# Decay matrices from a stationary mask, scores computed with the chunk matrices, modulation sums gathered by 32x32 transposes, and tokens loaded first

## The chip, the core and the metric

The kernel runs as one program on one core of a Trainium2 chip. The metric is the device time of one execution in microseconds (us), the median of several runs. The engines of the core are named as in the profile: PE (matrix multiplication; PEld is its weight load), DVE (vector), ACT (activation), POOL (GpSimd), SP (it only issues DMAs here), and sixteen DMA engines that all queues share.

## The reference, cut to what matters

Two layers over 256 latent tokens and 256 context tokens of width 2048, all in float32. Layer 0 mixes by eight gated-DeltaNet heads, in both directions of time, beside eight neighbourhood-attention heads; layer 1 mixes by a short gated convolution. Each layer ends in a SwiGLU network with 5632 hidden columns. Before each mixer and each SwiGLU the tokens are normalised and modulated by rows that come from a condition vector.

```python
sh1, sc1, g1, sh2, sc2, g2 = jnp.split(jax.nn.silu(c) @ ada_w[l] + ada_b[l], 6, axis=-1)
h = modulate(x_lat, norm_mix[l], sh1, sc1)
...
# gated delta rule, chunks of tokens (g, beta: one value per token and head, in two directions)
gc = jnp.cumsum(g, axis=-1)
decay = jnp.exp(jnp.where(lower_incl, gc[..., :, None] - gc[..., None, :], -jnp.inf))
m = jnp.where(i[:, None] > i[None, :], jnp.einsum('bhnid,bhnjd->bhnij', kb, k) * decay, 0.0)
t_inv = lax.linalg.triangular_solve(eye + m, ...)                 # inverse of each chunk's matrix
...
a_intra = jnp.where(lower_incl, jnp.einsum('bhnid,bhnjd->bhnij', q, k) * decay, 0.0)
# scan over chunks: v_new = u - w S;  S' = S exp(g_last) + k_dec^T v_new;  o = q_dec S + a_intra v_new
...
s_loc = jnp.einsum('brqhd,brjkhd->bhrqjk', qg, kg) * scale + bias # neighbourhood attention, bias from rpb
```

The context tokens give only the start state of the delta rule and extra keys and values; the output is the latent stream.

## The kernel before, in words

**Numbers.** A float32 product of large matrices is made from three products of "float32r" parts: each weight block of 128 x 1024 is copied to `whi` (ACT) and the rest subtracted into `wlo` (DVE), and the tokens are held as a high and a low part as well. `tm_stream` (tokens stationary, weights moving in 512 columns, lines 291 to 302) and `fm_stream` (weights stationary, 256 tokens moving, lines 317 and 321) run such a product over sixteen (or 44) blocks `k` of 128 rows. One `k` is one "step". Small products of the delta rule use plain float32 matmuls.

**Order.** Each engine runs its own instructions in a fixed order. That order is written at build time by a planner (`schedule_with_timeline_sim=True`), which plays the program through with its own estimates of durations and takes what the program names first. `Pump` draws a certain number of steps of a side job for each step of a stream. `plan` holds four pieces of the delta rule that are put into the program at the step numbers of `P_INV`; steps are counted over the streams QB (2 x 16 steps), KB and VB (2 x 32 steps).

**The start.** `start_block(b)` (b from 0 to 7) loads 4.2 MB of layer 0's modulation weights into four `araw0` tiles and sums them over the condition vector on PE (line 533). `token_stats` loads all tokens (`xn`, 4.2 MB, line 569), takes squares on ACT and scales by the root mean square on DVE (line 576). `start_tokens(b)` turns the sums into shift and scale of two blocks of 128 features, transposes the tokens' features, modulates them and splits them into `h_hi` and `h_lo`; the first two streams (`C_KA`, through `both`) take two steps each beside every block.

**The delta rule.** `gates` makes `g_t`, `beta` and their exponentials. `decay(d, tt, q)` gives exp of the sums of `g` between two tokens of a chunk for four heads: a mask times `g_t` (DVE, line 834), four float32 matmuls against the opposite mask (line 838), exp on ACT (line 840). `chunk_matrices(seq)` is called for the context (`seq` 1) and, inside `second_inverse`, for the latents (`seq` 0): it makes k.k products (`pG`, line 870), times decay and beta (`nt`, line 874), cuts out the 32x32 diagonal blocks (`dgs`: DVE transposes, line 880, and ACT copies), the off-diagonal ones (POOL copies, line 884, and ACT copies), and solves all diagonal blocks at once by 31 dependent pairs of DVE operations; the result goes through a DRAM tile `dz` and comes back as `xd` and `xdT`. `inverses` joins them by small matmuls (lines 962 to 979). `latents`, at step `P_INV[3]`, calls the second inverse of the latents, then `latent_scores(q)` for two groups of four heads (q.k products, line 1070, eight more calls of `decay`, two DVE products each, lines 1073 and 1074, into `AT`), then `latent_quad(q)`, which runs `scan` (lines 1000 to 1044).

**Beside and after it.** Eight attention heads (`na_scores`, `na_values`, lines 1180 to 1212); each head first loads its bias rows `br` (two DMAs, one buffer) and adds the band mask into `bq` (DVE, line 1183). The stream ZA follows, whose result `zst` goes to the DRAM tile `zd` by a DMA on SP (line 1220). `latent_out(q)` normalises the delta rule's output and splits it into `yhi`, `ylo`. The stream of `ev_w_out` takes its sixteen `k` in the order `YO` = (2, 0, 1, 3): attention heads 0 to 3, delta heads 0 to 3, delta heads 4 to 7, attention heads 4 to 7.

**Later modulation.** `ada_job` adds weight rows times the condition into `acc` (128 x 1024, DVE, line 346), one row block per step, beside the streams of SwiGLU 0 (8 column blocks), of layer 1's mixer (4) and SwiGLU 1 (2). At the end of a block it sums `acc` over the 128 partitions: `acc` is split into `ah` (ACT) and `al` (DVE), sixteen matmuls with the one-column mask `pick` (line 355) give 8 x 128 sums, ACT copies them, and for the kinds "sh" and "sc" a transpose turns them back to columns.

Of the kernel before, what the change touches and what calls it, by code (L numbers as in the profile page):

```python
# [42 lines left out]
P_INV = (30, 32, 79, 80)  # L43
# [65 lines left out]
def body(tc, x, c, ctx, c_ctx, ada_w, ada_b, norm_mix, norm_ffn, ffn_w_gate, ffn_w_up, ffn_w_down,  # L109
# [224 lines left out]

    def ada_job(pool_, l, seg, kind, gamma=None):

        wr = ada_w[l].rearrange("(k p) n -> p k n", p=128)
        for blk in range(2):
# [11 lines left out]
            ah = pool_.tile([128, 1024], F32R, name="ah", tag="ah", bufs=1)  # L350
            al = pool_.tile([128, 1024], F32R, name="al", tag="al", bufs=1)
            split(ah, al, acc, DVE)
            for f in range(8):
                for a in (ah, al):
                    PE.matmul(p[0:8, 0:128], pick[:, 7 - f:15 - f], a[:, f * 128:(f + 1) * 128],
                              start=f == 0 and a is ah, stop=f == 7 and a is al)
# [5 lines left out]
            pc = smt()  # L362
            transpose(pc[:, 0:8], g)
            ada_done(l, seg, kind, gamma, fs_, pc[:, 0:8])
# [344 lines left out]

    sums = start_block(0)  # L710
    token_stats()
# [106 lines left out]
    gates()  # L818
    abstk.close()
# [11 lines left out]
    def decay(d, tt, q):  # L831

        gm = g2("gm")
        DVE.tensor_tensor(gm, C(("gt", "lt")[d])[:, None, :].to_broadcast([128, 4, 128]),
                          g_t[:, d, tt, q * 4:q * 4 + 4, None].to_broadcast([128, 4, 128]), op=OP.mult)
        pD = gdt()
        for i in range(4):
            PE.matmul(pD[:, i * 128:(i + 1) * 128], gm[:, i, :], C(("le", "ge")[d]), start=True, stop=True)
        em = g2("em")
        ACT.activation(em, pD.rearrange("p (i e) -> p i e", i=4), AF.Exp)  # L840
        return em
# [11 lines left out]
    def chunk_matrices(seq):  # L853
# [6 lines left out]
        for q in range(2):  # L860
# [3 lines left out]
            SP.dma_start(kTd[:, seq, q * 4:q * 4 + 4, :], kT)  # L864
            for ti in range(2):
                tok = slice(ti * 128, ti * 128 + 128)
                nt = gw.tile([128, 2, 4, 128], F32, name="nt", tag="lsol", bufs=1)
                pG = gdt()
                for i in range(4):
                    PE.matmul(pG[:, i * 128:(i + 1) * 128], kT[:, i, tok], kT[:, i, tok], start=True, stop=True)  # L870
                for d in range(2):
                    em = decay(d, t0 + ti, q)
                    for i in range(4):
                        DVE.scalar_tensor_tensor(nt[:, d, i, :], pG[:, i * 128:(i + 1) * 128],
                                                 beta[:, d, t0 + ti, q * 4 + i:q * 4 + i + 1], em[:, i, :],
                                                 op0=OP.mult, op1=OP.mult)
# [626 lines left out]
```

## Time and profile before

| | |
|---|---|
| median of 3 runs | 2819.64 us (2818.58 to 2827.38) |
| the profiled execution: its own time | 2823.79 us |
| its span (first to last instruction) | 2822.0 us |
| mean granted clock of PE | 0.989 |
| PE busy | 2719.8 us (96%) |
| DVE busy | 1920.1 us (68%) |
| ACT busy | 1301.9 us (46%) |
| POOL busy | 50.3 us (2%) |
| DMA | 680.78 MB, mean 241 GB/s |

Rough map of the span, by the first and last start of lines in the trace: the start to about 160 us; delta-rule preparation and the streams KA, QA and VA to about 388 us; QB, KB, VB, ZA, attention, scans and `ev_w_out` to about 925 us; SwiGLU 0 to about 1685 us; layer 1's mixer to about 2065 us; SwiGLU 1 to the end.

How to read the rows: a row of a timeline gives start, duration, engine, line, operation, output<-inputs, shape and count, and in brackets how long the engine was idle before and what ended that. A group row gives count, busy time in all, mean of one in ns, then idle time before. A row of a tile gives minimum, median and maximum in ns and the first and last start. A row of stretches gives busy time of each engine with its instruction count, then the granted PE clock, the DMA engines' busy share, and GB/s. A matmul's recorded duration includes its way through the array; what a matmul costs in a full queue is the distance from one start to the next.

### The profile page before, as it was taken

The numbers are of one execution on the slowest core, as the hardware profiler recorded it, in microseconds if no ns is written. First come the engines' busy times: TensorE is split into PE (matmuls) and PEld (weight loads), VectorE is DVE, ScalarE is ACT, GpSimd is POOL, SyncE is SP. The second block draws the span as 40 slices with busy tenths as digits, with TensorE's granted clock in tenths as the row PEclk, the third lists the DMA queues.
The fourth block names the chain that finished last, engine by engine and source line by source line (L and its number), as shares of the span: only waits on it lengthen the run. The fifth ranks groups of instructions, "written<-read, shape, count | busy, mean of one in ns | idle before, by whom it ended". The sixth has DMA issues, their size and how long they took to land.

```text
span 2822.0 us, 40405 instructions
## 1 busy us (share of the span) xinstructions
PE 2719.8 (96%) x15113; PEld 2277.5 (81%) x15113; DVE 1920.1 (68%) x2647; ACT 1301.9 (46%) x1943; POOL 50.3 (2%) x77
## 2 busy tenths in 40 slices
PE   5999989999999999999999999999999999999998
PEld 3799989887778788888888878878878888888886
DVE  2377768866767888776678667797678644445665
ACT  2267534322454544444455555444454444444554
POOL 0000100000000000000000000000000000000000
PEclk9999999999999999999999999999999999999999
DMA  9945578887758699987788647998559766656663
GB/s 342 325 135 157 148 234 259 270 250 226 213 200 285 208 333 340 345 291 255 264 283 286 197 154 275 333 327 286 186 196 326 247 193 186 187 188 215 190 192 126
DMA packets 286399, 680.78 MB, mean 241 GB/s; under 512 B 57209, under 2 KB 100833, under 8 KB 284795
## 3 DMA queue, kind: packets, MB, share of 16 engines
q1 hardware_dynamic: 281828, 668.73, 71.3%
q10 hardware_dynamic: 4375, 9.48, 0.9%
q8 instruction: 118, 1.93, 0.3%
q14 instruction: 78, 0.64, 0.1%
HBM read 657.63 MB, written 20.48 MB: 240 GB/s over the span
## 4 chain that ended last, share of the span: by engine, by line
PE 78%; DMA 10%; DVE 6%; ACT 3%; issue 2%; SPq 1%; DVEq 0%; POOL 0%; ACTq 0%
PE mm L294 19%; PE mm L291 19%; PE mm L292 19%; PE mm L321 7%; DMA araw<-in_ada_w_dram 5%; PE mm L300 2%; PE mm L301 2%; PE mm L302 2%; DVE wlo L243 2%; PE sm L191 2%; DMA raw<-in_od_w_in_dram 1%; PE sm L533 1%; DVE acc L346 1%; DVE acc L389 1%; PE gd L321 1%
## 5 line engine op out<-in xcount | busy, mean ns | idle before, releaser
L243 DVE TENSOR_TENSOR wlo<-raw,whi 128x1024 fp32r<-128x1024 f32 x800 | 971.1, 1222 | 436.8 <-ACT whi L172 430.9
L172 ACT ACTIVATE whi<-raw 128x1024 fp32r<-128x1024 f32 x800 | 842.2, 1059 | 825.6 <-PE mm L294 618.9
L292 PE MATMUL mm<-wlo,fhi 128*128 128x512 f32 x1232 | 472.4, 392 | 0.0
L291 PE MATMUL mm<-whi,fhi 128*128 128x512 f32 x1232 | 470.7, 396 | 0.0
L294 PE MATMUL mm<-whi,flo 128*128 128x512 f32 x1232 | 392.2, 392 | 0.1
L346 DVE SCALAR_TENSOR_TENSOR acc<-araw,cT,acc 128x1024 f32<-128x1024 f32 x224 | 287.3, 1283 | 130.2 <-DMA araw<-in_ada_w_dram 123.5
L294 PEld LDWEIGHTS mm<-whi,flo 128*128 128x128 f32 x1232 | 230.8, 188 | 51.1 <-DVE flo L1288 0.5
L292 PEld LDWEIGHTS mm<-wlo,fhi 128*128 128x128 f32 x1232 | 231.8, 188 | 48.7
L291 PEld LDWEIGHTS mm<-whi,fhi 128*128 128x128 f32 x1232 | 231.9, 188 | 48.2
L291 PE MATMUL mm<-whi,ahi 128*128 128x512 f32 x672 | 259.8, 392 | 0.0
L292 PE MATMUL mm<-wlo,ahi 128*128 128x512 f32 x672 | 259.3, 391 | 0.0
L294 PE MATMUL mm<-whi,alo 128*128 128x512 f32 x672 | 209.8, 392 | 0.0
L321 PE MATMUL mm<-hllo,whi 128*128 128x256 f32 x608 | 172.9, 289 | 0.0
L321 PE MATMUL mm<-hlhi,whi 128*128 128x256 f32 x570 | 161.7, 292 | 2.2 <-DVE hlhi L561 1.9
L175 ACT ACTIVATE ahi<-prodT 128x256 fp32r<-128x256 f32 x176 | 73.2, 417 | 194.6 <-PE mm L292 183.9
L389 DVE SCALAR_TENSOR_TENSOR acc<-araw,cT,acc 128x512 f32<-128x512 f32 x192 | 142.7, 747 | 29.1 <-DMA araw<-in_ada_w_dram 27.3
L321 PE MATMUL mm<-hlhi,wlo 128*128 128x256 f32 x570 | 157.8, 289 | 0.0
L292 PEld LDWEIGHTS mm<-wlo,ahi 128*128 128x128 f32 x672 | 126.2, 188 | 27.7
L294 PEld LDWEIGHTS mm<-whi,alo 128*128 128x128 f32 x672 | 126.1, 188 | 27.3
L291 PEld LDWEIGHTS mm<-whi,ahi 128*128 128x128 f32 x672 | 126.2, 188 | 27.1
L292 PE MATMUL mm<-wlo,dhi 128*128 128x512 f32 x336 | 126.4, 396 | 2.2 <-DVE wlo L243 2.2
L291 PE MATMUL mm<-whi,dhi 128*128 128x512 f32 x336 | 123.8, 397 | 0.6 <-DVE u_t L1428 0.6
(419 smaller groups left out, 4194.0 us busy)
## 6 DMA issues: line engine op xcount, KB each, us to landing
araw<-in_ada_w_dram SPq DMA_DIRECT2D x288, 512.0 KB
raw<-in_ffn_w_down_dram SPq DMA_DIRECT2D x176, 512.0 KB
raw<-in_ffn_w_gate_dram SPq DMA_DIRECT2D x160, 512.0 KB
raw<-in_ffn_w_up_dram SPq DMA_DIRECT2D x160, 512.0 KB
raw<-in_ev_w_in_dram SPq DMA_DIRECT2D x112, 512.0 KB
araw<-in_ada_w_dram SPq DMA_DIRECT2D x192, 256.0 KB
raw<-in_od_w_in_dram SPq DMA_DIRECT2D x96, 512.0 KB
raw<-in_ev_w_out_dram SPq DMA_DIRECT2D x32, 512.0 KB
```

The costliest lines, as they stand in the source:

```text
L172: ACT.activation(dst, src, AF.Copy)
L175: ACT.activation(hi, src, AF.Copy)
L191: return PE.transpose(dst, src, ident[:n, :n])
L243: last_lo[0] = DVE.tensor_tensor(lo, raw, hi, op=OP.subtract).ins
L291: PE.matmul(ps[ti][n], a, hi[:, n * 512:(n + 1) * 512], start=first, stop=False)
L292: PE.matmul(ps[ti][n], a, lo[:, n * 512:(n + 1) * 512], start=False, stop=False)
L294: last_mm[0] = PE.matmul(ps[ti][n], b, hi[:, n * 512:(n + 1) * 512], start=False, stop=False).ins
L300: PE.matmul(ps[ti][n], lh(t), hi[:, c_], start=False, stop=False)
L301: PE.matmul(ps[ti][n], lh(t), lo[:, c_], start=False, stop=False)
L321: last_mm[0] = PE.matmul(ps[f][:, n * 256:(n + 1) * 256], wt, mv(w, k), start=False, stop=i == len(ks) - 1 and g == len(group) - 1 and j = ...
L346: DVE.scalar_tensor_tensor(acc, raw, cT[:, k:k + 1], acc, op0=OP.mult, op1=OP.add)
L389: DVE.scalar_tensor_tensor(accs[n], raws.pop(i), cT[:, k:k + 1], accs[n], op0=OP.mult, op1=OP.add)
```

## The change

- **Tokens ahead.** `token_stats()` stands before `start_block(0)`.
- **Decay.** `g_t` is split once into `g_hi` and `g_lo` (float32r), and the two masks are copied to `past`. Each `decay` now makes two products of mask and `g` (one on DVE, one on POOL, float32r) and two float32r matmuls of 512 columns with `past` as the stationary part.
- **Scores with the chunk matrices.** `latent_scores` is gone. `chunk_matrices(0)` makes the q.k products beside its k.k products and uses the same decays, so 24 calls of `decay` become 16, and two loads of `kT` go; the load of `qT` moves with it. The decays are made before `pG`.
- **Steps.** `P_INV` goes from (30, 32, 79, 80) to (34, 36, 84, 86).
- **Later modulation.** `sum_parts` replaces split and `pick` matmuls: a DVE transpose of `acc` within 32x32 blocks, a DVE sum over 32, and four float32 matmuls of 8 columns with the mask `fold`. Kinds "sh" and "sc" need no transpose any more; "row" has one more copy and one transpose.
- **Attention bias.** `br` is gone, `bq` has three buffers and the mask is added in place.
- **ZA.** `zst` is written to `zd` from POOL's queue instead of SP's.

```diff
-P_INV = (30, 32, 79, 80)
+P_INV = (34, 36, 84, 86)
...
+    def sum_parts(dst, pool_, acc, n, tag, bufs):
+        at = pool_.tile([128, 4 * n, 32], F32, name="accT", tag=tag, bufs=bufs)
+        ar = pool_.tile([128, n, 4], F32, name="accR", tag="accR", bufs=bufs)
+        DVE.transpose(at.rearrange("p b r -> p (b r)"), acc)
+        DVE.tensor_reduce(ar.rearrange("p k b -> p (k b)"), at, axis=AX.X, op=OP.add)
+        for b in range(4):
+            PE.matmul(dst[b * 32:b * 32 + 32, 0:n], C("fold"), ar[:, :, b], start=True, stop=True)
...  (in ada_job)
-            split(ah, al, acc, DVE)
-            for f in range(8):
-                for a in (ah, al):
-                    PE.matmul(p[0:8, 0:128], pick[:, 7 - f:15 - f], a[:, f * 128:(f + 1) * 128],
-                              start=f == 0 and a is ah, stop=f == 7 and a is al)
-            g = pool_.tile([16, 128], F32, name="grow", tag="grow", bufs=1)[0:8]
-            acopy(g, p[0:8, 0:128])
+            sum_parts(p, pool_, acc, 8, "accT", 1)
             if kind == "row":
+                gc = pool_.tile([128, 8], F32, name="gcol8", tag="gcol8", bufs=1)
+                acopy(gc, p[:, 0:8])
+                pc = smt()
+                transpose(pc[0:8, 0:128], gc)
+                g = pool_.tile([16, 128], F32, name="grow", tag="grow", bufs=1)[0:8]
+                acopy(g, pc[0:8, 0:128])
...
-    sums = start_block(0)
     token_stats()
+    sums = start_block(0)
...
+    split(g_hi, g_lo, g_t)
+    for d in range(2):
+        acopy(past[:, d, :], C(("gt", "lt")[d]))
...  (in decay)
-        DVE.tensor_tensor(gm, C(("gt", "lt")[d])..., g_t[...].to_broadcast([128, 4, 128]), op=OP.mult)
-        for i in range(4):
-            PE.matmul(pD[:, i * 128:(i + 1) * 128], gm[:, i, :], C(("le", "ge")[d]), start=True, stop=True)
+        for i, (g_, e_) in enumerate(((g_hi, DVE), (g_lo, POOL))):
+            gm = gw.tile([128, 4, 128], F32R, name="gm", tag="m2", bufs=G2)
+            e_.tensor_tensor(gm, C(("le", "ge")[d])..., g_[...].to_broadcast([128, 4, 128]), op=OP.mult)
+            PE.matmul(pD, past[:, d, :], gm.rearrange("p i e -> p (i e)"), start=not i, stop=bool(i))
...  (in chunk_matrices)
+            if not seq:
+                qT = load_feat("qT", qTd[:, q * 4:q * 4 + 4, :], lg, 1)
+                ATs.append(lg.tile([128, 16, 128], F32, name="AT", tag="AT", bufs=2))
...
+                ems = [decay(d, t0 + ti, q) for d in range(2)]
...
+                if not seq:
+                    pK = gdt()
+                    for i in range(4):
+                        PE.matmul(pK[...], kT[:, i, tok], qT[:, i, tok], start=True, stop=True)
+                    for d, em in enumerate(ems):
+                        DVE.tensor_tensor(em, em, C(("le", "ge")[d])..., op=OP.mult)
+                        DVE.tensor_tensor(ATs[q][...], pK..., em, op=OP.mult)
...
-        ATs = [latent_scores(q) for q in range(2)]
...  (in na_scores)
-        bq = nap.tile([128, 6, 64], F32, name="bq", tag="bq", bufs=2)
-        br = nap.tile([128, 6, 64], F32, name="br", tag="br", bufs=1)
+        bq = nap.tile([128, 6, 64], F32, name="bq", tag="bq", bufs=3)
-            SP.dma_start(br[half * 64:half * 64 + 64], src)
+            SP.dma_start(bq[half * 64:half * 64 + 64], src)
-        DVE.tensor_tensor(bq, br, bandf..., op=OP.add)
+        DVE.tensor_tensor(bq, bq, bandf..., op=OP.add)
...  (in za_evac)
-        SP.dma_start(zd[:, ti, n * 512:(n + 1) * 512], o)
+        POOL.dma_start(zd[:, ti, n * 512:(n + 1) * 512], o)
```

More of the change, by code (lines that the diff above doesn't have):

```diff
@@ L831, in decay @@
     def decay(d, tt, q):
-        gm = g2("gm")
-        DVE.tensor_tensor(gm, C(("gt", "lt")[d])[:, None, :].to_broadcast([128, 4, 128]),
-                          g_t[:, d, tt, q * 4:q * 4 + 4, None].to_broadcast([128, 4, 128]), op=OP.mult)
         pD = gdt()
-        for i in range(4):
-            PE.matmul(pD[:, i * 128:(i + 1) * 128], gm[:, i, :], C(("le", "ge")[d]), start=True, stop=True)
+        for i, (g_, e_) in enumerate(((g_hi, DVE), (g_lo, POOL))):
+            gm = gw.tile([128, 4, 128], F32R, name="gm", tag="m2", bufs=G2)
+            e_.tensor_tensor(gm, C(("le", "ge")[d])[:, None, :].to_broadcast([128, 4, 128]),
+                             g_[:, d, tt, q * 4:q * 4 + 4, None].to_broadcast([128, 4, 128]), op=OP.mult)
+            PE.matmul(pD, past[:, d, :], gm.rearrange("p i e -> p (i e)"), start=not i, stop=bool(i))
         em = g2("em")
@@ L870, in chunk_matrices @@
                     PE.matmul(pG[:, i * 128:(i + 1) * 128], kT[:, i, tok], kT[:, i, tok], start=True, stop=True)
-                for d in range(2):
-                    em = decay(d, t0 + ti, q)
+                for d, em in enumerate(ems):
                     for i in range(4):
@@ L876, in chunk_matrices @@
                                                  op0=OP.mult, op1=OP.mult)
+                if not seq:
+                    pK = gdt()
+                    for i in range(4):
+                        PE.matmul(pK[:, i * 128:(i + 1) * 128], kT[:, i, tok], qT[:, i, tok], start=True, stop=True)
+                    for d, em in enumerate(ems):
+                        DVE.tensor_tensor(em, em, C(("le", "ge")[d])[:, None, :].to_broadcast([128, 4, 128]), op=OP.mult)
+                        DVE.tensor_tensor(ATs[q][:, d * 8 + ti * 4:d * 8 + ti * 4 + 4, :],
+                                          pK.rearrange("p (i e) -> p i e", i=4), em, op=OP.mult)
                 n0 = q * 8 + ti * 4
@@ L1059, in body @@
     lg = pool("gdn_lat", stack=lga, side="right")
-    def latent_scores(q):
-        qT = load_feat("qT", qTd[:, q * 4:q * 4 + 4, :], lg, 1)
-        kT = load_feat("kT", kTd[:, 0, q * 4:q * 4 + 4, :])
-        AT = lg.tile([128, 16, 128], F32, name="AT", tag="AT", bufs=2)
-        for ti in range(2):
-            tok = slice(ti * 128, ti * 128 + 128)
-            pK = gdt()
-            for i in range(4):
-                PE.matmul(pK[:, i * 128:(i + 1) * 128], kT[:, i, tok], qT[:, i, tok], start=True, stop=True)
-            for d in range(2):
-                em = decay(d, ti, q)
-                DVE.tensor_tensor(em, em, C(("le", "ge")[d])[:, None, :].to_broadcast([128, 4, 128]), op=OP.mult)
-                DVE.tensor_tensor(AT[:, d * 8 + ti * 4:d * 8 + ti * 4 + 4, :],
-                                  pK.rearrange("p (i e) -> p i e", i=4), em, op=OP.mult)
-        return AT
     def latent_quad(q, xdT, AT):
```

14 lines of the change are left out of this document (7 added, 7 removed).

## The prediction

> **What bounds the kernel now.** I read the page first, then stretches of the span, then the tiles of the edited lines.
>
> ```profile
> PE 2719.8 (96%) x15113; PEld 2277.5 (81%) x15113; DVE 1920.1 (68%) x2647; ACT 1301.9 (46%) x1943; POOL 50.3 (2%) x77
> PE 78%; DMA 10%; DVE 6%; ACT 3%; issue 2%; SPq 1%; DVEq 0%; POOL 0%; ACTq 0%
> ```
>
> PE carries the chain of work that ended last. A high busy share does not prove a full engine, since recorded matmuls overlap, so I look at the distance between starts where SwiGLU 0 runs and one modulation block closes:
>
> ```profile
> 1028.17 0.39 PE L291 MATMUL mm<-whi,fhi 128*128 128x512 f32 x1
> 1028.40 0.39 PE L292 MATMUL mm<-wlo,fhi 128*128 128x512 f32 x1
> ...
> 1028.86 0.22 PE L355 MATMUL sm<-ah,pick 128*8 128x128 f32 x1
> ...
> 1029.76 0.22 PE L355 MATMUL sm<-al,pick 128*8 128x128 f32 x1
> 1029.82 0.45 PE L292 MATMUL mm<-wlo,fhi 128*128 128x512 f32 x1
> ```
>
> A 512-column matmul costs 0.23 us, and no gap shows here: PE time taken out of this stage shortens the span. The second view is the stretch in which the edited delta-rule code lies (all engines):
>
> ```profile
> 520.00:540.00 20.00, 20.00 (x115) 17.40 (x114) 18.88 (x42) 5.71 (x12) 0.53 (x1) 1.00 0.51 174
> 680.00:700.00 20.00, 15.84 (x77) 11.97 (x75) 9.90 (x14) 4.38 (x5) 0.00 (x0) 0.99 0.73 180
> 700.00:720.00 20.00, 17.45 (x77) 13.22 (x77) 15.37 (x28) 7.30 (x14) 0.00 (x0) 0.84 0.75 226
> 760.00:780.00 20.00, 16.99 (x105) 14.59 (x104) 13.51 (x33) 12.67 (x23) 0.00 (x0) 1.00 0.65 189
> 800.00:820.00 20.00, 18.45 (x130) 16.20 (x128) 13.00 (x37) 6.09 (x21) 0.00 (x0) 1.00 0.37 129
> 820.00:840.00 20.00, 15.43 (x69) 11.76 (x69) 12.86 (x43) 14.67 (x53) 0.21 (x1) 0.83 0.15 51
> ```
>
> From 520 on DVE is nearly full (18.88 of 20 us); between 680 and 840 nothing is, and PE goes idle. What PE lacks at the end of it shows in the same stretches for the stream of `ev_w_out` alone (the matmuls that read `yhi`):
>
> ```profile
> 780.00:800.00 20.00, 8.85 (x28) 5.12 (x28) 0.41 (x1) 0.40 (x1) 1.00 0.95 348
> 800.00:820.00 20.00, 0.00 (x0) 0.00 (x0) 0.00 (x0) 0.00 (x0) 1.00 0.37 129
> 820.00:840.00 20.00, 0.02 (x1) 0.05 (x1) 2.17 (x5) 2.01 (x5) 0.83 0.15 51
> 840.00:860.00 20.00, 14.48 (x52) 9.68 (x53) 2.17 (x4) 1.77 (x3) 1.00 0.91 315
> ```
>
> The stream starts, stops for 40 us, and goes on at 840. It has used attention heads 0 to 3 and waits for the delta heads, whose scans run late:
>
> ```profile
> L1074 DVE TENSOR_TENSOR AT<-gd,em x8: 676/686/693, 656.6 to 722.5; 128x512 f32<-128x512 f32 x8
> L1042 PE MATMUL gd<-vn,AT x64: 271/275/377, 734.4 to 820.9; 128*128 128x128 f32 x64
> ```
>
> The latents' scores take from 656.6 to 722.5, and the scans that use them come after, until 820.9.
>
> **The change part by part.** *Decay.*
>
> ```profile
> 217.92 1.06 PE L838 MATMUL gd<-cs,gm 128*128 128x128 f32 x8
> 218.73 0.36 PE L321 MATMUL mm<-hlhi,wlo 128*128 128x256 f32 x1
> ...
> L834 DVE TENSOR_TENSOR gm<-cs,g_t x24: 678/684/692, 213.5 to 711.6; 128x512 f32<-128x512 f32 x24
> L840 ACT ACTIVATE em<-gd x24: 575/598/599, 219.1 to 715.8; 128x512 f32<-128x512 f32 x24
> ```
>
> The four float32 matmuls are recorded as eight and hold PE for 218.73 - 217.92 = 0.81 us; 24 calls cost 19.4 us. After: 16 calls of two 512-column matmuls, 16 x 0.46 = 7.4 us. PE saves 12.1 us at most; I take 11, as some scores lie where PE idles, and 6 as the poor end (half of it hidden). DVE loses 8 x 0.684 = 5.5 us, ACT 8 x 0.6 = 4.8 us; neither is counted, for they hide under PE in most of it. The split of `g_t` and two mask copies are four small instructions, once: nothing.
>
> *The product on POOL.* No row shows POOL multiplying. The nearest:
>
> ```profile
> L884 POOL COPY n<-nt 32x128 f32<-32x128 f32 x32 | 16.1, 505 | 325.6 <-DVE nt L874 324.9
> L381 POOL MEMSET acc<- 128x512 f32 x12 | 6.3, 528 | 363.0 <-DVE o_t L1095 168.2 <-PE sm L396 160.8 <-ACT junk L573 31.8
> 243.48 1.70 POOL L884 COPY n<-nt 32x128 f32<-32x128 f32 x2 [6.99 <-DVE nt L874]
> ```
>
> 512 elements written take 0.53 us; 128 copied take 0.505, so 512 read and written up to 2.0. DVE's own product runs beside it (0.68), so 0 to 1.3 us more per decay before the second matmul may start, 0 to 21 us for 16. What stands behind that matmul on PE is a weight stream, placed by the planner's own estimate, and POOL's `n32` copies stand ahead of the next product. I take 1.2 us for a product (the middle of the two rows, since it both reads and writes), 0.5 exposed, a third of it on the path: +3.
>
> The Trainium skill (GPSIMD Engine Reference, section 3.1) gives about 2.6 cycles an element for a two-input operation, an estimate of 1.1 us for 512 at its 1.2 GHz; by that the sum keeps its +3.
>
> *Scores with the chunk matrices.* DVE gets 8 products with the mask and 8 into `AT`, 16 x 0.68 = 10.9 us, into the stretch before and around 520, where it has 1.1 us free in 20. The q.k matmuls only move. Two loads of `kT` (0.5 MB each) go; `qT` is loaded on SP between `kTd` and the next weights, and its second load waits for the first group's q.k products, with weight loads queued behind: four `raw` buffers cover that, nothing. The diagonal solve ends up to 11 us later and the inverse stands 5 steps later (79 to 84), each 12 matmuls of 0.23 = 2.8 us, so 14 us of grace; but the whole piece also starts four steps later, in QB and KB. Ends 0 and +13 (11 plus half a stretch of slow clock); I take +3.
>
> *The late stage.* With scores done early the scans can follow the second inverse, whose last matmul starts here:
>
> ```profile
> L969 PE MATMUL gd<-xdT,Y x384: 191/194/267, 416.9 to 648.4; 32*32 32x32 f32 x128, 64*64 64x64 f32 x64
> ```
>
> At the new place that is 6 steps, 17 us, later: 665. The scans took 734.4 to 820.9; starting near 670 they end near 760 and no longer stop `ev_w_out`. What can be regained, from the stretches: idle PE of 4.2 + 2.5 (680 to 720), 3.0 (760 to 780) and 1.6 + 4.6 (800 to 840), and a slow clock of 0.16 and 0.17 of 20 us, 6.6: 22.5 us. More lies under the records of 800 to 840: 199 matmuls at 0.13 (the eight of 1.06 us above) are 26 us of work in 40, so 14 idle where the busy column says 6.2: 31 us in all. Part is due to the bias rows:
>
> ```profile
> 696.13 0.56 DVE L1183 TENSOR_TENSOR bq<-br,cs 128x384 f32<-128x384 f32 x1 [5.74 <-DMA br<-in_ev_rpb_dram]
> 697.88 0.50 PE L292 MATMUL mm<-wlo,hlhi 128*128 128x512 f32 x1 [2.27 <-DVE wlo L243]
> DVE bq L1183 <- DMA br<-in_ev_rpb_dram: 14.6, 4, 5.7
> ACT whi L172 <- DMA raw<-in_ev_w_out_dram: 11.5, 5, 6.0
> ```
>
> DVE stands 5.74 us before a bias row that could not be loaded ahead, and PE behind it. Three buffers end that (14.6 us of DVE waits in four). The `zd` write leaves SP, where the loads of `ev_w_out` stand behind it; on POOL only clears of `acc` do. I take 20 of the 31 us: the eight attention heads still run one behind another and late comes next their last head, which `ev_w_out` needs for its last four blocks. Ends: 0 and -31.
>
> *Later modulation.* Sixteen `pick` matmuls cost 1029.82 - 1028.86 = 0.96 us of PE. Four float32 matmuls of 8 columns, two passes each, cost between almost nothing and 8 x 0.1 (the row of eight above): 0.5 by the 0.06 spacing of the `pick` ones, whose weights are small too. The transposes saved by 8 blocks and added by 6 cancel. 14 x 0.46 = 6.4: I take -6, ends 0 and -13. DVE trades one subtraction for a transpose and a sum:
>
> ```profile
> L880 DVE STREAM_TRANSPOSE dgs<-nt 32x128 f32<-32x128 f32 x32 | 9.7, 302 | 0.4
> L1192 DVE TENSOR_REDUCE m<-sm 128x1 f32<-128x512 f32 x14 | 9.5, 683 | 2.2 <-PE sm L1188 2.2
> DVE wlo L243 <- ACT whi L172: 430.9, 368, 9.7
> ```
>
> For 1024 elements that is 1.2 to 2.4 and 1.3 us against 1.22: one to two and a half us more per block, covered by DVE's waits for `whi` (430.9 us); uncovered 14 x 2 = 28 us.
>
> *Tokens ahead.*
>
> ```profile
> 45.43 2.08 PE L317 MATMUL mm<-h,whi 128*128 128x512 f32 x4
> ...
> 20.00:40.00 20.00, 5.95 (x26) 2.89 (x22) 6.97 (x13) 12.67 (x13) 1.01 (x2) 1.00 1.04 392
> 40.00:60.00 20.00, 18.46 (x118) 12.40 (x119) 8.54 (x19) 4.17 (x8) 0.00 (x0) 1.00 1.09 354
> 100.00:120.00 20.00, 20.00 (x168) 16.48 (x167) 7.62 (x21) 5.75 (x9) 0.00 (x0) 1.00 1.00 320
> 120.00:140.00 20.00, 20.00 (x168) 14.35 (x166) 8.48 (x20) 5.00 (x9) 0.00 (x0) 1.00 1.05 333
> ```
>
> The first stream matmul stands at 45.43 and may come about 10 us earlier, as squares and scaling then lie under the weights' landing. But the DMA engines are full from 20 on, the same bytes must land before the eighth block, and that block ends the start. So only dips count: 354 against 320 and 333 is 10% and 6% of 20 us, 3 us. I take -2, ends -7 and +2.
>
> **The sum.** -11 + 3 + 3 - 20 - 6 - 2 = -33 against the profiled execution's 2823.8 us: 2791. That execution lies 4.2 us above the median of 2819.6, so against the median 2787.
>
> **The rivals.** *The late stage gives all.* Scans and heads both end early, PE never idles: -31 and -9 for modulation, -12 for decays, -4 start, with the two costs: -50, 2770. For it: `ev_w_out` stands still for 40 us. Against: DMA runs at 315 GB/s and over once it goes on, near the 354 of the start.
>
> *The attention heads bind instead.* If the last head ends as late as now, only the bias wait (6) comes back: -33 + 14 = -19, 2801. For it: the heads are last in `YO`. Against: they share DVE and banks with the scans.
>
> *Nothing is left.* The planner's new order loses about what the matmuls save, the change does not do what it says for the late stage, and POOL costs 10: 2816.
>
> *POOL holds DVE up, and the inverses come late.* Copies of 128 elements took 0.85 us each at 243.48, 3.4 for 512. At 4 us a product, with DVE standing still for it, chunk matrices grow by 8 x 4 + 11 - 14 = 29 us for the latents and 32 - 9 for the context (grace: two steps of QB and two of KB): PE, which runs in order, waits 52 us at the inverses, instead of my +6: 2787 + 46 = 2833. It decides from about 3.5 us a product. Against: DVE's products run at 0.684 with POOL busy 2% only, and the mean copy is 0.505.
>
> The Trainium skill (SBUF — State Buffer, Who interferes with whom) says that a DVE instruction with two SBUF inputs and a POOL instruction that reads SBUF lock each other out for a whole instruction; no run here shows a full lock yet.
>
> **How the numbers follow.** A measurement tells 0.3% (8.5 us) from no change: 2811 to 2828. Chances: my forecast 0.42 (2787, own range 2776 to 2798), all of the late stage 0.20 (2770), heads bind 0.22 (2801), nothing 0.10 (2816), POOL 0.06 (2833). Faster: the first three less their tail, 0.81; same 0.12; slower 0.07. The range leaves out the last two and the low tail: 2760 to 2811.
>
> **What would show it.** Right: products on POOL near 1.2 us; the last scan matmul starting before 780; the stream of `ev_w_out` without an empty stretch; no DVE wait for bias rows; SwiGLU 0 shorter by 3 to 4 us; the first stream matmul near 35 us but the eighth block hardly earlier. Wrong: PE waiting at the inverses (lines 962 on) for more than now, POOL products over 2 us, or attention heads ending after 830.

## The result, and the profile after

The changed kernel takes 2833.66 us (median of eight runs, 2831.56 to 2839.62) against 2825.08 of the kernel before on the same chip; the ratio of the runs' means is 1.0038, 95% interval 1.0025 to 1.0050. That is 0.4% slower; 2787 us, 1.2% faster, was forecast. The profiled execution has a span of 2829.8 us against 2822.0.

The page's first part, of the changed kernel:

```profile
PE 2707.7 (96%) x14839; PEld 2256.9 (80%) x14839; DVE 1934.7 (68%) x2654; ACT 1290.3 (46%) x1926; POOL 71.9 (3%) x97
```

PE lost 274 instructions and 12 us of busy time, and still the span grew: PE waits more. The stretches of 20 us (all engines: PE, PEld, DVE, ACT, POOL, then granted clock, DMA share, GB/s):

```profile
520.00:540.00 20.00, 19.65 (x105) 16.08 (x104) 19.71 (x45) 7.23 (x16) 5.54 (x10) 1.00 0.57 202
680.00:700.00 20.00, 18.48 (x92) 14.12 (x93) 8.73 (x16) 9.26 (x22) 0.00 (x0) 1.00 0.80 218
700.00:720.00 20.00, 14.04 (x66) 11.07 (x64) 10.89 (x21) 5.91 (x12) 0.00 (x0) 0.91 0.65 189
760.00:780.00 20.00, 14.10 (x78) 11.40 (x76) 6.03 (x14) 4.31 (x8) 1.25 (x2) 0.99 0.86 260
820.00:840.00 20.00, 15.02 (x69) 11.20 (x68) 13.70 (x47) 16.48 (x55) 0.00 (x0) 0.83 0.21 66
```

DVE is fuller at 520 (19.71), and the holes of the late stage have not closed: 14.04 at 700 (17.45 before) and 14.10 at 760 (16.99 before). Over the eight stretches from 680 to 840, PE is busy for 135.4 us where it was busy for 143.7: its recorded idle time has grown from 16.3 to 24.6 us. The stream of `ev_w_out` alone, and the last scans (first row) and heads (second row), with their first and last start:

```profile
780.00:800.00 20.00, 7.43 (x24) 4.83 (x24) 0.42 (x1) 0.48 (x1) 0.84 0.55 158
800.00:820.00 20.00, 2.28 (x8) 1.43 (x8) 0.42 (x1) 0.43 (x1) 1.00 0.53 188
820.00:840.00 20.00, 0.00 (x0) 0.00 (x0) 1.26 (x3) 1.32 (x4) 0.83 0.21 66
840.00:860.00 20.00, 12.61 (x45) 8.22 (x45) 3.19 (x5) 2.56 (x5) 1.00 0.81 290
```

```profile
L1067 PE MATMUL gd<-vn,AT x64: 271/275/520, 697.3 to 822.3; 128*128 128x128 f32 x64
L1218 PE MATMUL sm<-PT,vb x56: 377/379/454, 725.5 to 841.3; 128*128 128x256 f32 x56
```

The scans start 37 us earlier than before (697.3 against 734.4) and end at the same time (822.3 against 820.9). The inverse that they need ends at 679.3, 31 us later than before. The stream stops again until past 840. The first matmul of SwiGLU 0 stands at 931.7 (929.2 before), the first of its down-projection at 1435.9 (1432.0), the last of the kernel's down-projections at 2815.0 (2807.7).

Where the 8 us are, by matmul starts: the stages up to SwiGLU 0 lost 2.5 us, although the decays' matmuls hold PE for 12 us less (7.4 for 19.4); layer 1's mixer gained 1.8; the two SwiGLU networks lost the rest, 4.8 us of it in their down-projections, which the change does not touch.

### The profile page after: what moved, and what is told of

It is laid out like the page before. It is cut to its first block, busy times and chain, and to the rows that moved or that the text cites. A ratio compares the mean times of both kernels' runs of the same rounds, so it can differ in the third digit from the quotient of the medians.

```text
span 2829.8 us, 39839 instructions
## 1 busy us (share of the span) xinstructions
PE 2707.7 (96%) x14839; PEld 2256.9 (80%) x14839; DVE 1934.7 (68%) x2654; ACT 1290.3 (46%) x1926; POOL 71.9 (3%) x97
## 5 line engine op out<-in xcount | busy, mean ns | idle before, releaser
L395 DVE SCALAR_TENSOR_TENSOR acc<-araw,cT,acc 128x512 f32<-128x512 f32 x192 | 147.4, 769 | 23.7 <-DMA araw<-in_ada_w_dram 21.9
L176 DVE TENSOR_TENSOR alo<-prodT,ahi 128x256 fp32r<-128x256 f32 x176 | 74.4, 424 | 83.3 <-PE mm L294 78.7
```

What stands on the lines that cost most here:

```text
L176: (eng or DVE).tensor_tensor(lo, src, hi, op=OP.subtract)
L395: DVE.scalar_tensor_tensor(accs[n], raws.pop(i), cT[:, k:k + 1], accs[n], op0=OP.mult, op1=OP.add)
```

## Experiments

Ratios are to the kernel before, with 95% intervals. By these intervals a difference of two ratios is uncertain by 0.17 to 0.26%, 5 to 7 us, and by 0.33% for the last pair, so most effects below stand little above that. Microseconds are ratio differences times 2822. "Order" is the order of instructions that the planner writes; most edits change it, also in stages that they do not touch.

**1. Placement of the stationary tiles.**

```diff
 e1_pad (on the changed kernel)
-ar = pool_.tile([128, n, 4], F32, name="accR", ...)
+ar = pool_.tile([128, 128], F32, name="accR", ...)[:, 0:4 * n]...
-gc = pool_.tile([128, 8], F32, name="gcol8", ...)
+gc = pool_.tile([128, 128], F32, name="gcol8", ...)[:, 0:8]
 e2_shift (on the kernel before)
 ap_ = pool(f"ffn_a{l}", stack=fs)
+POOL.memset(ap_.tile([128, 16], F32, name="shift64"), 0.0)
 f4_place64 (on e7_dve, below)
-ar = pool_.tile([128, 128], ...)
+ar = pool_.tile([128, 144], ...)
```

> The changed kernel with its two small new modulation tiles rounded up to 512 bytes a partition (computation unchanged). Theory A (placement): accR (128 bytes) and gcol8 (64 bytes) push the tiles allocated behind them, ahi and alo among them, to an odd multiple of 64 bytes, and TensorE takes the down-projections' stationary tiles more slowly from there (mean distance of matmul starts 232.4 ns against 228.9 before, some 1056 matmuls in each of two layers). Then the distance goes back to 228.9, each down-projection gets 3 to 4 us shorter, and the time falls by about 7 us to 2827. Rival B (order): the slower pace comes from the new order of DVE and ACT work in that stage; then padding changes nothing there and the time stays within 2 us of 2833.7.

> The kernel before with one more 64-byte tile in the pool that stands ahead of prodT, sg, ahi and alo in both SwiGLU layers, and nothing else. Theory A (placement): the matmul starts of both down-projections go from 228.9 to about 232.4 ns, and the time rises by about 7 us, to 2832. Rival B (order): distance and time unchanged, within 1 us of 2825.

> As e7_dve, the same order of instructions on every engine, with accR's padding 64 bytes longer, so that prodT, sg, ahi and alo lie 64 bytes further on. Placement (three points so far: the pool ahead of them 0 bytes past a multiple of 512, 229.1 ns between matmul starts in the second down-projection; 64 bytes, 226.9; 192 bytes, 232.5): if the place alone sets the pace, 226.9 ns again, 2.2 ns x 2112 matmuls = 4.6 us less, about 2806. Rival: the 226.9 ns belonged to the kernel before and its old tiles; then no change from e7_dve.

e1_pad 1.0010 (0.9997 to 1.0023), e2_shift 0.9986 (0.9976 to 0.9995), f4_place64 0.9934 (0.9915 to 0.9953) against 0.9954 of e7_dve. e1_pad has the changed kernel's instructions in the changed kernel's order on every engine. The effect of the 64 bytes in f4_place64 is inside the uncertainty; the pace of the matmuls shows it more sharply. The matmuls that read `ahi` (two of three of the stream) in 200 us of the second down-projection, one row each of the kernel before, the changed kernel, e1_pad, e2_shift and f4_place64:

```profile
2580.00:2780.00 200.00, 156.90 (x584) 109.57 (x584) 31.01 (x73) 29.98 (x72) 1.00 0.61 194
```

```profile
2580.00:2780.00 200.00, 156.43 (x575) 107.82 (x573) 30.87 (x73) 29.99 (x72) 1.00 0.59 191
```

```profile
2580.00:2780.00 200.00, 157.54 (x584) 109.30 (x583) 30.61 (x73) 30.39 (x73) 1.00 0.60 193
```

```profile
2580.00:2780.00 200.00, 157.57 (x590) 110.38 (x588) 31.44 (x74) 30.85 (x74) 1.00 0.62 195
```

```profile
2580.00:2780.00 200.00, 157.54 (x590) 110.36 (x588) 31.02 (x73) 30.42 (x73) 1.00 0.56 184
```

That is 584, 575, 584, 590 and 590 at a full clock. Over the whole second down-projection, pauses left out, the starts of the stream's matmuls lie 229.1, 232.5, 229.1, 226.9 and 226.9 ns apart. The pool ahead of these tiles holds 20,992, 17,088, 17,920, 21,056 and 17,984 bytes a partition: 0, 192, 0, 64 and 64 past a multiple of 512. The pace follows the place: the changed kernel and e1_pad have one order and two paces, and the same pace comes with different orders. I had the sign of e2_shift wrong: 64 bytes more make the stream faster, not slower; what costs is the change's 192. The placement costs the changed kernel 0.28%, 8 us; 3.4 ns x 2112 matmuls are 7 us of it. Why 64 is good and 192 bad is open; the tiles' own addresses were not read.

**2. Bias rows in place.**

```diff
 e5_br (on the changed kernel)
-bq = nap.tile([128, 6, 64], F32, name="bq", tag="bq", bufs=3)
+bq = nap.tile([128, 6, 64], F32, name="bq", tag="bq", bufs=2)
+br = nap.tile([128, 6, 64], F32, name="br", tag="br", bufs=1)
...
-DVE.tensor_tensor(bq, bq, bandf...)
+DVE.tensor_tensor(bq, br, bandf...)
```

> The changed kernel with the bias rows as before: loaded into br (one buffer), added into bq (two buffers), instead of added in place in three buffers. Theory C (bias waits): in place, DVE stands before all eight bias rows, 35.9 us in all against 14.6 before, and the scans' R and the softmax behind it in DVE's queue hold PE; then the DVE wait falls to 15 us or less, the last scan matmul comes well before 822, and the time falls by 6 to 12 us. Rival D (heads bind): the attention heads run one behind another from the end of their key and value streams whatever DVE waits for, so the last PT,vb matmul stays at 838 to 842 and the time within 3 us of 2833.7.

1.0009 (0.9997 to 1.0021): 8 us less than the changed kernel. Waits of the changed kernel, then of e5_br:

```profile
DVE bq L1190 <- DMA bq<-in_ev_rpb_dram: 35.9, 8, 6.6
ACT zst L1224 <- DMA zd<-zst: 12.6, 1, 12.6
```

```profile
DVE bq L1191 <- DMA br<-in_ev_rpb_dram: 19.1, 4, 6.3
```

What it does to PE, in three timelines of the changed kernel (SP's queue, DVE, PE):

```profile
709.38 1.28 SPq L1187 DMA_DIRECT2D bq<-in_ev_rpb_dram  x2
```

```profile
719.77 0.56 DVE L1190 TENSOR_TENSOR bq<-bq,cs 128x384 f32<-128x384 f32 x1 [6.29 <-DMA bq<-in_ev_rpb_dram]
...
721.30 1.12 DVE L1028 SCALAR_TENSOR_TENSOR R<-gd,negegc,vtok 128x128 f32<-128x128 f32 x4
```

```profile
717.28 0.39 PE L292 MATMUL mm<-wlo,hlhi 128*128 128x512 f32 x1
721.79 2.04 PE L1045 MATMUL gd<-R,xdT 128*128 128x128 f32 x8 [4.13 <-DVE R L1028]
...
781.80 2.07 PE L1053 MATMUL gd<-vd,ktok 128*128 128x128 f32 x8 [5.73 <-ACT vd L1049]
```

The load is issued at 709.38 and there at 719.8, 10 us later. DVE stands 6.29 us before it, the scan's R waits behind it in DVE's queue, and PE waits 4.13 us for R. At 770 it goes on: the `zst` product is held by the bias row, so the `zd` write starts late, ACT's next `zst` waits 12.6 us for it to land, and PE waits 5.73 us for `vd`, which stands behind that on ACT. With three buffers the sum could be put right behind its load; with two it came late enough for the load to be there in half of the cases. In the changed kernel all eight sums start 7 to 10 us behind the issue of their load; in e5_br the last four start 15 to 25 us behind it. Neither pause is in e5_br. So theory C has the time (8 us of its 6 to 12) and the wait of PE right. It missed the size of DVE's wait (19.1 us, not 15) and the end of the scans (823.5, not well before 822); and the heads end no earlier (843.9), as rival D said.

**3. The new modulation.**

```diff
 e3_pick (on the changed kernel): ada_job as before
-sum_parts(p, pool_, acc, 8, "accT", 1)
+split(ah, al, acc, DVE)
+...  16 pick matmuls, copy, transpose
```

> The changed kernel with the later modulation gathered as before (split and pick matmuls), all other edits kept. It takes away the new transposes and sums on DVE and, with its old tiles, the 64-byte shift. Theory: the new modulation costs, in all: 7 us for the shift, and at SwiGLU 0 its 2.45 us on DVE at each block's end (against 1.2) holds the sg products and with them PE, which about eats the 6 us of matmuls saved; so the time falls by 5 to 8 us, to about 2827, and the remaining 2 us or so are the even layer's. Rival: the modulation as predicted gains 6 us; then this kernel is slower than the changed one, 2840.

1.0045 (1.0029 to 1.0061). The theory, a fall of 5 to 8 us, does not hold. The rival expected 6 us more than the changed kernel; the 2 us measured cannot be told from none. e3_pick has the old placement, so it compares with e1_pad: 0.35%, 10 us slower (uncertain by 6). The new gathering gains that much, and the 192 bytes that it brought along took 8 of them back. My reason for "eats" was a real wait, though, on DVE and on PE in the changed kernel:

```profile
1021.84 1.25 DVE L340 STREAM_TRANSPOSE accT<-acc 128x1024 f32<-128x1024 f32 x1
1023.01 1.18 DVE L243 TENSOR_TENSOR wlo<-raw,whi 128x1024 fp32r<-128x1024 f32 x1
1024.12 1.21 DVE L341 TENSOR_REDUCE accR<-accT 128x32 f32<-128x1024 f32 x1
1025.24 2.48 DVE L1377 TENSOR_TENSOR sg<-mm,sg 128x512 f32<-128x512 f32 x4
```

```profile
1025.98 0.44 PE L191 MATMUL sm<-cs,sg 128*128 128x128 f32 x2 [2.14 <-DVE sg L1377]
```

Where a block closes just as a column block ends, the `sg` products stand behind transpose and sum, and PE waits 2.14 us. In e1_pad, same order, this pause is not there, and the gate and up streams of SwiGLU 0 take 498.8 us (504.2 in the changed kernel's profile, 502.8 before).

**4. POOL or DVE for the low part.** c0_pad_br is the changed kernel with corrections 1 and 2.

```diff
 c0_pad_br = e1_pad + e5_br
 e7_dve (on c0_pad_br); d_dve, d_pool: the new decay alone on the kernel before
-for i, (g_, e_) in enumerate(((g_hi, DVE), (g_lo, POOL))):
+for i, (g_, e_) in enumerate(((g_hi, DVE), (g_lo, DVE))):
```

> The changed kernel with both corrections: small modulation tiles rounded to 512 bytes, bias rows through br as before. Theory: the two act in different stages (down-projections, attention heads), so they add: each took about 8 us off alone (ratios 1.0010 and 1.0009 against 1.0038), together the ratio to the kernel before comes to 0.998, about 2817 us, with the distance of matmul starts in the down-projections at 229 ns and the DVE wait for bias rows below 15 us. Rival: the two measure the same run-to-run shift; then the ratio stays at 1.001.

> As c0_pad_br, with the low part's mask product of the decays on DVE instead of POOL. Theory F (POOL late): the product takes 1.27 us on POOL against 0.68 on DVE, and the second matmul, which waits for it, holds PE in its order: then DVE's version gains 1 to 5 us. Rival G (DVE full): between 480 and 620 DVE is busy 19 to 20 of 20 us, 16 more products are 11 us more there, and the time rises by 2 to 8 us. The prediction took POOL's cost as 3 us.

> The kernel before with the new decay alone, both products on DVE (24 calls, scores and steps as before). Prediction's term: 19.4 us of float32 matmuls fall to 24 x 0.46 = 11 us of PE, 8.4 less, of which half to all shows: 4 to 8 us faster than before, about 2816. Rival G (DVE full): 24 products more on DVE, 16 us in stretches where it is nearly full, take it back: 0 to 5 us slower. Rival H (order): anything within 10 us, from the order that comes out for the late stage.

> As d_dve, with the low part's product on POOL. Theory F (POOL costs by itself): slower than d_dve by some 8 us or more (24 products instead of 16). Theory H (order): the difference to d_dve has another size or sign, and in the profile no PE wait over 1 us stands before a decay's second matmul. The prediction's +3 lies between.

c0_pad_br 0.9983 (0.9971 to 0.9996): the two corrections add (DVE's wait for bias rows, expected below 15 us, is 18.5). e7_dve 0.9954 (0.9936 to 0.9972), d_dve 0.9982 (0.9968 to 0.9996), d_pool 1.0005 (0.9991 to 1.0019). The decay alone gains 5 us, as expected of d_dve; with POOL the kernel is 6 us slower there (8 or more were expected) and 8 us slower in e7_dve's pair, each uncertain by 6. The products, and two of them that met (the changed kernel):

```profile
L849 DVE TENSOR_TENSOR gm<-cs,g_hi x16: 677/683/1528, 216.1 to 528.4; 128x512 fp32r<-128x512 f32 x16
L849 POOL TENSOR_TENSOR gm<-cs,g_lo x16: 1038/1268/1987, 216.3 to 528.0; 128x512 fp32r<-128x512 f32 x16
```

```profile
487.07 1.22 DVE L243 TENSOR_TENSOR wlo<-raw,whi 128x1024 fp32r<-128x1024 f32 x1
488.20 1.53 DVE L849 TENSOR_TENSOR gm<-cs,g_hi 128x512 fp32r<-128x512 f32 x1
```

```profile
487.32 1.86 POOL L849 TENSOR_TENSOR gm<-cs,g_lo 128x512 fp32r<-128x512 f32 x1 [2.84 <-DVE AT L900]
```

DVE's 0.68 becomes 1.53 beside POOL's, and POOL's 1.04 becomes 1.86: POOL's starts while DVE's subtraction runs, and DVE's product, started at 488.20, ends 0.55 us after POOL's end at 489.18. Summed over the DVE instructions that overlap a POOL product, DVE loses 8 us, of the 11 us (16 x 0.68) that the move spares it. But in the changed kernel no wait of PE over 0.6 us is put down to a product, so theory F's wait is not seen. And e7_dve's profile (one execution each) is ahead of c0_pad_br's by 2.3 us before the first decay, by 4.6 at 530 us, behind the last one, and by 9.7 at SwiGLU 0: most of the gain lies where there is no decay, for with the product on DVE the planner also orders the other stages otherwise. Rival G, a slower kernel with more work on DVE, falls. That the kernels with POOL's product are slower is measured twice; how much of it is the two products in each other's way and how much the order stays open.

**5. Scores, steps of the inverses.**

```diff
 e9_scores (on c0_pad_br): scores in latents() as before
-P_INV = (34, 36, 84, 86)
+P_INV = (30, 32, 79, 80)
 e6_pinv (on c0_pad_br), f1_dve_pinv (on e7_dve)
-P_INV = (34, 36, 84, 86)
+P_INV = (30, 32, 84, 86)
```

> As c0_pad_br, with the latents' scores made where the kernel before made them, after the second inverse, all four inverses at the steps before (30, 32, 79, 80), and the new decay everywhere (so 24 calls of it instead of 16). Theory D (heads bind): attention heads run from the end of the context's streams to about 840 whichever way the scans are fed, so scores made early gain nothing there, while they put 11 us of DVE work and 30 us of delay in front of the inverses: the time falls by 3 to 8 us. Rival (the prediction's late stage): scans start 30 us later without the early scores, the stream of ev_w_out stops longer, and the time rises by 10 to 20 us.

> As c0_pad_br, with the two context inverses back at stream steps 30 and 32 (the latents' stay at 84 and 86). Theory E (uncovered loads): the weight loads of the stream queue on SP behind the sixteen xd and xdT loads at 402 to 413, the stream starves, and in the kernel before the first inverse's small matmuls filled that hole (PE gap 3.2 us at 418, in the changed kernel 7.9 to 9.7 at 414 to 418, with a longer half-clock stretch behind it). Back at step 30 the gap falls to about 3 us and the time by 4 to 7 us. Rival: the diagonal solve ends later now, the inverse waits for its xd and the stream behind it; no gain, or 3 us lost.

> As e7_dve (both corrections, both products of a decay on DVE), with the context inverses at steps 30 and 32. e6_pinv gained 9 us over c0_pad_br by its runs, though its profile shows the same PE gap at 421 (8.1 us). Theory E' (a real gain by earlier context inverses): here too 4 to 9 us, to about 2804. Rival H (order): every edit gives the planner another order of the late stage, good or bad by up to 10 us, and the gains of e6_pinv and e7_dve are two such draws: then this one may land anywhere from 2806 to 2822, and the stretch from the 100th to the 120th weight split, not that around step 30, is where it differs.

e9_scores 1.0021 (1.0005 to 1.0037): 0.38%, 11 us slower than c0_pad_br (uncertain by 6). Theory D, 3 to 8 us faster, falls. The 11 us belong to early scores with what comes along: 16 calls of `decay` instead of 24 (8 x 0.46 = 3.7 us of PE) and the later steps of the inverses. The two other runs show what steps alone can do. e6_pinv 0.9957 (0.9943 to 0.9972), 7 us faster; f1_dve_pinv 0.9987 (0.9973 to 1.0001), 9 us slower than e7_dve by the same edit. Two signs for one edit, and the pause that theory E names is there in both (8.0 and 7.2 us; 8.7 in c0_pad_br): E and E' fall, H stands, except that the stretch that differs most in f1 is the one between the 80th and 100th weight split. The profile of e6_pinv is that of its slowest run (2821.94 us; the median is 2810.82), so it cannot show where the gain lies.

**6. Start and zd.**

```diff
 f2_tokens (on e7_dve)
-token_stats()
 sums = start_block(0)
+token_stats()
 f3_zdsp (on e7_dve)
-POOL.dma_start(zd[...], o)
+SP.dma_start(zd[...], o)
```

> As e7_dve, with the start as in the kernel before (the first modulation block ahead of the tokens' loads). Theory I (the start loses): with tokens ahead the first stream matmul comes at 39 instead of 45, but the 24th weight split stood at 212 to 215 in the changed kernels against 210 to 211 before, so the early start is given back twice over; then this kernel's 24th split comes 2 to 4 us earlier and the time falls by 2 to 4 us. Rival (prediction: gains 2, between -7 and +2): the time rises by 2 us.

> As e7_dve, with the zd writes on SP's queue again. The prediction counted the move to POOL as part of the late stage's gain without a number of its own. Theory J: ACT's zst waits once for a zd write that POOL issues late (12.6 us in the changed kernel), which costs the late stage 1 to 3 us: the time falls by that. Rival: SP's weight loads stand behind the writes, the time rises by 1 to 3 us; within 3 us it cannot be told from a new order.

f2_tokens 0.9929 (0.9914 to 0.9945): tokens ahead cost 7 us (uncertain by 7; but all four runs, 2798.90 to 2805.31 us, lie below the four of e7_dve on the same chip, 2808.57 to 2811.96). The rows of the modulation's last step (first and last start) in the changed kernel and in f2_tokens:

```profile
L552 PE MATMUL sm<-cs,mrow x64: 166/251/374, 34.7 to 147.4; 128*128 128x2 f32 x64
```

```profile
L552 PE MATMUL sm<-cs,mrow x64: 166/251/374, 23.4 to 147.2; 128*128 128x2 f32 x64
```

The first block is ready 11 us later with the tokens ahead, the eighth at the same time: the same bytes. The early first stream matmul (39.0 against 44.8 us) only moves work to where it must wait, and the 25th weight split comes at 212.5 in e7_dve, 210.7 in f2_tokens, the 49th at 355.2 and 350.2. The rest of the 7 us lies in later stages and may be order. f3_zdsp 0.9941 (0.9925 to 0.9957) is 4 us better than e7_dve, within the uncertainty of such a difference.

**7. What paces the late stage.** best is e7_dve with f2, f3 and f4 together.

```diff
 h_heads (on best, without f4's 64 bytes): heads 4 to 7 left out
-for h in range(8):
+for h in range(4):
 h_scan (likewise): the second quad's latent scan left out
-o_ts.extend(latent_quad(q, xdTs[q], ATs[q]) for q in range(2))
+o_ts.extend([latent_quad(0, xdTs[0], ATs[0])] * 2)
```

> The four findings together: e7_dve with the start as before, the zd writes on SP, and the 64-byte placement of ahi and alo. Single effects against e7_dve (0.9954): tokens -0.25%, zd -0.13%, placement -0.20%. Theory: tokens and placement add and zd's is within the noise: 0.991 of the kernel before, about 2796 us. Rival: the tokens' gain and zd's are draws of the order and do not add: 0.993.

> As best, but attention heads 4 to 7 are left out (their places in yhi3 and ylo3 are filled with copies of heads 0 to 3). Theory D (heads pace the late stage: 17 to 18 us a head from 686 on, 826 at the end, whatever the scans do): the last PT,vb matmul comes 45 to 70 us earlier, and the even layer ends (first matmul that reads fhi, 916 in best) as soon as the scans and their output let it, 15 to 35 us earlier. Rival (scans pace it): the last scan matmul stays at 809 and the layer's end moves by less than 8 us.

> As best, but the latents' scan of the second four delta heads is left out (the first four heads' result is used in its place). Theory D (heads): the last PT,vb matmul stays within 6 us of 826 and the layer's end within 10 us of 916, though 3.5 us of matmuls for each of the scan's steps are gone. Rival (scans): the scans end some 50 us earlier and the layer's end moves by 15 us or more.

h_heads takes 2788.88, h_scan 2785.90 us (two runs each). Heads, scans and the first matmul of SwiGLU 0, in best, h_heads and h_scan:

```profile
L1219 PE MATMUL sm<-PT,vb x56: 379/379/454, 713.9 to 825.9; 128*128 128x256 f32 x56
L1067 PE MATMUL gd<-vn,AT x64: 271/275/377, 701.1 to 809.2; 128*128 128x128 f32 x64
L291 PE MATMUL mm<-whi,fhi x1232: 388/392/775, 916.3 to 2534.7; 128*128 128x512 f32 x176
```

```profile
L1219 PE MATMUL sm<-PT,vb x32: 379/379/382, 710.2 to 763.8; 128*128 128x256 f32 x32
L1067 PE MATMUL gd<-vn,AT x64: 271/275/377, 698.3 to 795.3; 128*128 128x128 f32 x64
L291 PE MATMUL mm<-whi,fhi x1232: 388/392/775, 896.3 to 2519.9; 128*128 128x512 f32 x176
```

```profile
L1219 PE MATMUL sm<-PT,vb x56: 379/379/766, 713.8 to 810.7; 128*128 128x256 f32 x56
L1067 PE MATMUL gd<-vn,AT x32: 271/275/275, 701.9 to 760.5; 128*128 128x128 f32 x32
L291 PE MATMUL mm<-whi,fhi x1232: 388/392/776, 902.1 to 2522.7; 128*128 128x512 f32 x176
```

Without four heads the layer ends 20.0 us earlier, without half of the scans 14.2. By the timeline's starts a head's matmul groups hold PE for about 4.8 us and the scan of four delta heads for about 16: 19 and 16 us were left out. So each gives back about its own matmul time and no more, while PE's recorded idle time from 680 us to that first matmul stays at 20.3, 23.8 and 20.6 us. For h_heads theory D's numbers came out (heads' end 62 us earlier, the layer's 20); h_scan, where it had the layer's end within 10 us and the heads' within 6, speaks against it with 14.2 and 15.2. The rival fails in h_heads, where it allowed 8 us. Neither chain paces the stage alone. What comes back is PE's own work; why some 20 us of waits stay in all three is open.

**8. The best version, and other stationary tiles.**

```diff
 g_fhi64 (on best; accR padded to 128 again)
 hp = pool(f"ffn_h{l}", stack=fs)
+POOL.memset(hp.tile([128, 16], F32, name="shift64"), 0.0)
 dp = pool("od", stack=ds)
+POOL.memset(dp.tile([128, 16], F32, name="shift64"), 0.0)
```

> As best, but the 64 bytes stand ahead of fhi and flo in both SwiGLU layers and ahead of dhi, dlo, zhi, zlo (and 0 more in the modulation pool, so that ahi and alo lie where they do in best). Theory (placement matters to every stationary tile): the distance of matmul starts falls from 230.4 to about 228 ns in the gate and up streams (2 x 2080 matmuls) and the od streams (1500), 10 to 14 us in all, to 2784. Rival (only the relation of ahi and alo's three-buffer ring to the weights matters): gate, up and od keep their pace and the time stays within 2 us of best; third, they get slower, 233 ns, and the time rises by 10 us: the present place is then the better one.

best 0.9899 (0.9877 to 0.9920), 2796.1 us: the three single gains add (0.9954 less 0.25, 0.13 and 0.20% is 0.9896). g_fhi64 0.9875 (0.9850 to 0.9900), 2787.95 us, has the lowest median of the complete kernels; its 0.24%, 7 us, are less than the 10 to 14 expected and inside the uncertainty of this pair. The pace shows the effect. Matmuls that read `fhi` in 440 us of SwiGLU 1, best and g_fhi64:

```profile
2060.00:2500.00 440.00, 348.26 (x1246) 231.91 (x1245) 2.23 (x4) 3.79 (x10) 1.00 0.70 225
```

```profile
2060.00:2500.00 440.00, 348.82 (x1254) 234.05 (x1253) 1.19 (x2) 0.88 (x2) 1.00 0.71 227
```

The distance of starts went from 230.2 to 228.1 ns there and from 230.6 to 229.0 in the od streams: placement matters to every group of stationary tiles tried. By the profiles' starts the two gate and up stages got 4 us shorter in all, the od mixer 3; the rest of the span's 9.8 us lies mainly in the first mixer (its end at 913.1 against 916.3), within what one order shows from one execution to the next.

## Why the prediction was wrong

The change as it stands, term by term. Each measured value is the difference of two ratios, with its pair.

| term | predicted | measured, us | from |
|---|---|---|---|
| decay in two matmuls | -11 | -5 (24 calls) | d_dve |
| product on POOL | +3 | +6 to +8 | d_pool, c0 against e7 |
| scores early | +3, and part of the -20 | -11 | e9 against c0 |
| bias rows in place | part of the -20 | +8 | changed kernel against e5 |
| zd on POOL | nothing of its own | +4, uncertain | e7 against f3 |
| later modulation | -6 | -10 | e3 against e1 |
| its placement | not seen | +8 | changed kernel against e1 |
| tokens ahead | -2, ends -7 and +2 | +7 | e7 against f2 |

They add to between +7 and +9 us; measured +11 (0.0038 x 2822). The sum fits more closely than it can prove: each term is uncertain by 5 to 7 us, they were measured on different kernels, and new orders alone moved the time by 7 and 9 us (experiment 5). Only the placement was measured at an unchanged order, and only for it and the bias rows do traces show the cost itself.

*The step that failed first is the late stage's -20.* It counted 31 us between 680 and 840 as idle or slow, and 20 as regained. None of it came back: PE's recorded idle time there rose from 16.3 to 24.6 us and the time at half clock from 13.7 to 20.5, and with every correction (best) the idle time is still 15.1. About 8 of the 31 us were never recorded as idle but came from an estimate of 0.13 us a matmul. What h_heads and h_scan gave back was the time of the matmuls left out, not idle time. Scores made early did let the scans start 37 us sooner, as said, but "starting near 670 they end near 760" took the scans for one chain behind the scores. The inverse ended at 679, not 665. And the scans share PE's order with the streams and heads, and were spread out until 822. The signs that I had named for this stage all came out against it: scans past 780, an empty stretch in the stream, heads to 841.

*The bias rows* were read wrongly. I saw a wait for a load "that could not be loaded ahead" and held that three buffers end it. More buffers also let the sum be put earlier in DVE's queue, and what stood behind it waited for the load too: 14.6 us became 35.9.

*POOL's product* was sized right (1.2 taken, 1.27 measured), its cost was not (+3 taken, +6 to +8 measured, order included). The rival "POOL holds DVE up" ended near the measured time by chance: its condition, 3.5 us a product, was not met. The Trainium skill (SBUF — State Buffer, Who interferes with whom) says that such a pair lock each other out for a whole instruction. In the pair shown the trace agrees with that rule: DVE's product took 1.53 us instead of 0.68 and ended only after POOL's.

*The modulation* was right in sign and low in size (-10 for -6). The sign named for it, SwiGLU 0 shorter by 3 to 4 us, shows in e1_pad (498.8 for 502.8), not in the changed kernel (504.2). What it did to the place of later tiles stood in no row of the trace before, and could have been asked about: the list of tiles that grow and shrink is in the diff.

*Tokens ahead*: that the eighth block does not move was right (147.4 against 147.2). That the early start then has no value was not in the sum. The first block's 11 us of delay may be the price; no run separates it from the order.

Rivals: "the attention heads bind" (2801) had the heads' end right, and the reason not: leaving out scans moved that end as well; "nothing is left" (2816) described the late stage best.

## What to carry to other kernels

Before counting an idle stretch as gain, ask whether its gaps belong to waits or to the changes between small matmul groups, and take away a part of the work to see what comes back. A buffer more does not only let a load start earlier; it lets the instruction behind the load move up in an in-order queue, and everything behind it then waits for the landing. When tiles change size, compare the pace of streams that the change does not touch: here they told of 8 us that no edited line explains.

## What the runs showed of the hardware

The place of a stationary tile in SBUF sets the pace of 512-column float32r matmuls at a full clock: 226.9, 229.1 or 232.5 ns a start, with the pool ahead of it 64, 0 or 192 bytes past a multiple of 512.

A pause of PE costs twice: it is idle, and a stretch at half clock follows most of them. In the changed kernel, behind the pause of 7.68 us that the stream has at 414:

```profile
413.23 0.28 PE L321 MATMUL mm<-hllo,whi 128*128 128x256 f32 x1
413.35 0.28 PE L321 MATMUL mm<-hlhi,wlo 128*128 128x256 f32 x1
...
422.48 0.41 PE L321 MATMUL mm<-hllo,whi 128*128 128x256 f32 x1
422.69 0.41 PE L321 MATMUL mm<-hlhi,whi 128*128 128x256 f32 x1
422.90 0.41 PE L321 MATMUL mm<-hllo,whi 128*128 128x256 f32 x1
```

Its stretch with the granted clock (the 0.80, third number from the end):

```profile
420.00:440.00 20.00, 17.90 (x180) 17.50 (x181) 13.87 (x16) 6.99 (x10) 0.00 (x0) 0.80 1.00 344
```

Matmuls that stood 0.12 us apart stand 0.21 apart behind it, and 0.12 again from 428.2 on. The granted clock's record has half clock from 417.9 to 428.1 here. It shows such stretches, 3.4, 6.8 or 10.2 us long, from 1 to 5 us after the start of most pauses of 2 us and more: nine (54.6 us) in the kernel before, twelve (71.7 us) in the changed one. The mean granted clock fell from 0.989 to 0.986. By half of the difference, an estimate, the changed kernel loses some 8 us more to the half clock; they are part of the terms in the table, not beside them. The Trainium skill (TensorE: Matmul & The Clock Gate, Part 1) has windows of 3.4 us with a half or a full clock, and in this the record agrees.

Two executions of the same order (the changed kernel and e1_pad, up to SwiGLU 0) reached its first matmul at 931.7 and 938.0 us: a single profile can't resolve a few microseconds there, and pairs of timed runs were needed.
